# Where split weights lie in their buffers: byte offset 64 everywhere, or 88 and 76

## The chip, the core and the metric

The kernel runs on one core of one Trainium2 chip. Its time is the device time of one execution in microseconds (us); the time before is the median of three runs. A profiled execution gives the trace; its span goes from the first to the last instruction and is a little shorter than the execution's own time.

## The reference

One layer of a decoder trunk on x of 256 positions by 1024 channels, float32:

```python
proj = x @ w_in                      # 1024 x 10240: ten groups of 1024 columns
a_x, a_gate, s_u, s_v, q, k, v, g_a, g_s, g_m = split(proj)
y_a = rg_lru(causal_dwconv(a_x)) * gelu(a_gate)
y_s = gelu(s_u) * (tril(w_s) @ layer_norm(gelu(s_v)) + b)
y_m = moba_attention(q, k, v)        # 8 heads of 128; one block of 256, so causal
m = sigmoid(g_a)*y_a + sigmoid(g_s)*y_s + sigmoid(g_m)*y_m
x = layer_norm(alpha*x + m @ w_out)
h = x @ w_up                         # 1024 x 6144
x = layer_norm(alpha*x + (gelu(conv3(h_gate)) * h_up) @ w_down)
```

## The kernel before

All weights are streamed once from HBM, in chunks of 1 MiB (128 partitions x 2048 float32): 40 of w_in, 4 of w_out, 24 of w_up and 12 of w_down. A chunk of w_in or w_up holds 256 output columns for all eight blocks of 128 input channels, so a row of a partition is eight pieces of 256 floats, one after the other (index k).

To keep float32 accuracy with TensorE's float32r type, each operand is split in two: `split` (lines 68 to 70) lets ScalarE (ACT) write hi, the rounded copy, and VectorE (DVE) write lo, the rest. A product is then three matmuls, hi by hi, hi by lo and lo by hi (`passes`, line 125). A chunk thus costs 8 x 3 matmuls for each of two halves, 48 matmuls of 256 columns.

There are two ways to use a chunk. Feature-major (`fm_pe`, line 219): the weights are the stationary operand, 128 columns at a time, and the activations of all 256 positions (xh, xl, or x1Th, x1Tl for w_up) stream through; the result has channels on partitions. Token-major (`tm_mm`, line 240): 128 positions of the activations are stationary, and 256 weight columns stream. Token-major are the groups S_V and V of w_in and the first two gate chunks of w_up (`first_gates`, tile p_tg); the other 32 chunks of w_in (tiles p_ax, p_su, p_ag, p_gm, p_q, p_k, p_ga, p_gs) and 22 of w_up (p_g, p_u) are feature-major. Every one of these matmuls needs a weight load (LDWEIGHTS) of its own, a row PEld in the trace. w_out and w_down chunks stream 512 columns, or 256 in the last pieces p_woq and p_dq, against stationary activations (`row_mm`, line 631).

A step is a matmul function, the chunks it uses and a function that handles its results. The main loop (line 1015) loads up to LOOK = 3 chunks ahead on SP's DMA queue, prepares a chunk with `prep`, issues the matmuls and then the rest of the step. The order of TensorE's work is the order in the code; in three stretches that of the other engines is too. There are five raw buffers of half a chunk, four hi and four lo buffers.

A hi or lo buffer has 2048 + PAD elements, and `prep` (line 103) puts the chunk `shift_of` bytes into it, 4 bytes an element:

```python
at = shift_of.get(i, 0) // 4
hi = his.tile([P, 2048 + PAD], F32R, ...)[:, at : at + 2048]
lo = los.tile([P, 2048 + PAD], F32R, ...)[:, at : at + 2048]
```

`shifted(i)` (line 236) sets 64 bytes for each chunk of w_in and w_up; w_out and w_down are not in the table and lie at 0, and the activations are not shifted. So the shift sets the distance in a partition between what the weight load reads and what the matmul streams.

Of the kernel before, what the change touches and what calls it, by code (L numbers as in the profile page):

```python
# [31 lines left out]
A_X, A_G, S_U, S_V, Q_, K_, V_, G_A, G_S, G_M = range(10)  # L32
# [10 lines left out]
LOOK = 3  # L43


SHIFT = 64
PAD = 256


# [1 line left out]
def trunk_kernel(ctx: ExitStack, tc, xw, x, w_in, wrg, wsT, w_out, w_up, w_down, rows, packed, out):  # L51
# [23 lines left out]
    def chunk(src):  # L75
        chunks.append(src)
        return len(chunks) - 1

    shift_of = {}
# [153 lines left out]
        acts = cur["acts"]  # L233
        return pe

    def shifted(i):
        shift_of[i] = SHIFT
        return i

    def tm_mm(c, dst, tok, ks, acts, ms=(0, 1, 2)):  # L240
# [20 lines left out]
    def wi(group, c):  # L261
        return chunk(w_in[group * 4 + c])
# [3 lines left out]
    vst = small.tile([P, 2, 4, 6], F32, name="vst", tag="vst", bufs=1)  # L266

    def sv_step(c):
        i = shifted(wi(S_V, c))

        def pe():
            if c > 1:
                p = bank(f"p_sv{c}")
                cur["p"] = [p[:, 0, :], p[:, 1, :]]
                tm_pe(i, p)
                return
            cur["p"] = [bank(f"p_sv{c}{tok}")[:, 0, :] for tok in range(2)]
            for k in range(KT + 1):
                for ks, ms in (((k,), (0,)), ((k - 1,), (1, 2))):
                    for tok in range(2):  # L280
                        if 0 <= ks[0] < KT:
                            tm_mm(i, cur["p"][tok], tok, ks, (xh, xl), ms)

        def post():
            cols = slice(c * S, (c + 1) * S)
            for tok in range(2):
                nc.scalar.activation(va[:, tok, cols], cur["p"][tok], AF.Gelu_apprx_tanh)
                nc.vector.bn_stats(vst[:, tok, c, :], va[:, tok, cols])
            if c == 3:
                gb = U("gb", (P, 2, D))  # L290
                load_row(gb[:, 0, :], 0)
                load_row(gb[:, 1, :], 1)
                for tok in range(2):
                    mv, rs = aggregate(vst[:, tok], f"sv{tok}")
                    normalise(va[:, tok, :], va[:, tok, :], mv, rs, gb[:, 0, :], gb[:, 1, :])

        step(pe, [i], post)
# [34 lines left out]
    xc = {}  # L332

    def ax_step(c):
        i = shifted(wi(A_X, c))

        def pe():
            cur["p"] = p = bank(f"p_ax{c}")
            fm_pe(i, p)()

        def post():
            p = cur["p"]
            if c == 0:
                xc["f"] = U("xc")
                xc["h"] = U("xch", dt=F32R)
                xc["l"] = U("xcl", dt=F32R)
            for j in range(2):
                conv(xc["f"][:, 2 * c + j, :], p[:, j, :], "cw", "cb", 2 * c + j, 8, 4)
            s = slice(2 * c, 2 * c + 2)
            split(xc["f"][:, s, :], xc["h"][:, s, :], xc["l"][:, s, :])  # L350

        step(pe, [i], post)
# [1 line left out]
    gu = {}  # L354

    def su_step(c):
        i = shifted(wi(S_U, c))

        def pe():
            cur["p"] = p = bank(f"p_su{c}")  # L360
            fm_pe(i, p)()

        def post():
            if c == 0:
                gu["f"] = U("gu")
            nc.scalar.activation(gu["f"][:, 2 * c : 2 * c + 2, :], cur["p"], AF.Gelu_apprx_tanh)

        step(pe, [i], post)
# [23 lines left out]
    ga = {}  # L392

    def ag_step(c):
        i = shifted(wi(A_G, c))

        def pe():
            cur["p"] = p = bank(f"p_ag{c}")
            fm_pe(i, p)()

        def post():
            if c == 0:
                ga["f"] = U("ga")
            nc.scalar.activation(ga["f"][:, 2 * c : 2 * c + 2, :], cur["p"], AF.Gelu_apprx_tanh)

        step(pe, [i], post)
# [42 lines left out]
    sgm = {}  # L449

    def gm_step(c):
        i = shifted(wi(G_M, c))

        def pe():
            cur["p"] = p = bank(f"p_gm{c}")
            fm_pe(i, p)()

        def post():
            if c == 0:
                sgm["f"] = U("sgm")  # L460
            nc.scalar.activation(sgm["f"][:, 2 * c : 2 * c + 2, :], cur["p"], AF.Sigmoid)

        step(pe, [i], post)
# [1 line left out]
    av = {}  # L465

    def v_step(c):
        i = shifted(wi(V_, c))

        def pe():  # L470
            cur["p"] = p = bank(f"p_v{c}")
            tm_pe(i, p)

        def post():
            if c == 0:
                av["h"] = U("avh", (P, 2, D), F32R)
                av["l"] = U("avl", (P, 2, D), F32R)
                av["r"] = U("avr", (P, D))
            s = slice(c * S, (c + 1) * S)
            split(cur["p"], av["h"][:, :, s], av["l"][:, :, s])  # L480
            nc.scalar.copy(av["r"][:, s], cur["p"][:, 1, :])

        step(pe, [i], post)
# [1 line left out]
    qk = {}  # L485

    def qk_step(which, c):
        i = shifted(wi(Q_ if which == "q" else K_, c))

        def pe():  # L490
            cur["p"] = p = bank(f"p_{which}{c}")
            fm_pe(i, p)()

        def post():
            if which == "q":
                qk[c] = U(f"qk{c}", (P, 4, 2, S), F32R)
            o = 0 if which == "q" else 2
            hl = (qk[c][:, o], qk[c][:, o + 1])
            split(cur["p"], *hl)
            first = tmp.tile([P, 2, P], F32, name=f"{which}f{c}", tag=f"{which}f")  # L500
            nc.scalar.copy(first, cur["p"][:, :, :P])
            qk[which, c] = (*hl, first)

        step(pe, [i], post)
# [76 lines left out]
    mg = {}  # L581

    def ga_step(c):
        i = shifted(wi(G_A, c))

        def pe():
            cur["p"] = p = bank(f"p_ga{c}")
            fm_pe(i, p)()

        def post():  # L590
            s = slice(2 * c, 2 * c + 2)
            t = tmp.tile([P, 2, S], F32, name=f"sga{c}", tag="t0")
            nc.scalar.activation(t, cur["p"], AF.Sigmoid)
            nc.vector.tensor_mul(ga["f"][:, s, :], ga["f"][:, s, :], t)

        step(pe, [i], post)

    def gs_step(c):
        i = shifted(wi(G_S, c))

        def pe():
            cur["p"] = p = bank(f"p_gs{c}")
            fm_pe(i, p)()

        def post():
            if c == 0:
                mg["h"] = U("mgh", dt=F32R)
                mg["l"] = U("mgl", dt=F32R)
            s = slice(2 * c, 2 * c + 2)
            t = tmp.tile([P, 2, S], F32, name=f"sgs{c}", tag="t0")  # L610
            nc.scalar.activation(t, cur["p"], AF.Sigmoid)
            nc.vector.tensor_mul(t, t, gu["f"][:, s, :])
            nc.vector.tensor_add(t, t, ga["f"][:, s, :])
            nc.vector.tensor_add(t, t, sgm["f"][:, s, :])
            split(t, mg["h"][:, s, :], mg["l"][:, s, :])

        step(pe, [i], post)
# [129 lines left out]
    def up_chunk(which, c):  # L747
        return chunk(w_up[c if which == "g" else 12 + c])
# [6 lines left out]
        pf["t", c] = t  # L755

    def up_step(which, c):
        i = shifted(up_chunk(which, c))

        def pe():  # L760
            pf[which, c] = bank(f"p_{which}{c}")
            cur["acts"] = res["hl"]
            fm_pe(i, pf[which, c])()

        def post():
            if which == "g":
                gate_post(c)
                return
            t = pf["t", c]
            nc.vector.tensor_mul(t, t, pf["u", c])  # L770
            act = U(f"act{c}", (P, 2, 2, S), F32R)
            pf["a", c] = (act[:, 0], act[:, 1])
            split(t, *pf["a", c])

        step(pe, [i], post)

    def first_gates():


        ids = [shifted(up_chunk("g", c)) for c in range(2)]  # L780
        pairs = [(2 * q, 2 * q + 1) for q in range(4)]

        def mm(c, tok, ks):
            tm_mm(ids[c], pf["tm", c][:, tok, :], tok, ks, res["hl"])

        def open_pe():
            for c in range(2):
                pf["tm", c] = bank(f"p_tg{c}")
            mm(0, 0, range(KT))

        step(open_pe, ids)
        for q in range(4):
            def pe(q=q):
                mm(1, 0, pairs[q])
                x1t_pe(1, q, psb)

            step(pe, ids, lambda q=q: x1t_post(1, q))

        def evacuate(c):
            t = tmp.tile([P, 2, 384], F32, name=f"tg{c}", tag="prob")[:, :, :S]  # L800
            nc.scalar.copy(t, pf["tm", c])
            pf["tg", c] = t

        step(lambda: [mm(0, 1, ks) for ks in pairs], ids, lambda: evacuate(0))
        step(lambda: [mm(1, 1, ks) for ks in pairs], ids, lambda: evacuate(1))
# [114 lines left out]
    for c in range(4):  # L920
        sv_step(c)
# [172 lines left out]
```

## Time and profile before

| what | value |
|---|---|
| time, median of 3 runs | 485.58 us (485.13 to 487.52) |
| profiled execution, its own time | 485.5 us |
| its span | 483.8 us, granted TensorE clock 0.996 |
| busy: PE (matmul) / PEld (weight load) | 473.5 us / 458.1 us |
| busy: DVE / ACT / POOL | 337.3 / 271.4 / 21.9 us |
| read from HBM | 91.31 MB, 191 GB/s over the span with what is written |

Matmuls are pipelined: the duration of one in the trace is longer than the time to the start of the next. The pace is therefore read from starts: the time from the first start of a piece to the first start of the next piece, divided by the matmuls in the piece (their number is from the code, 48 per chunk; the counts of a window also hold those that only reach into it).

### The profile page before, as it was taken

What the parts mean: (1) busy time and instruction counts of PE and PEld (TensorE: products, weight loads), DVE (VectorE), ACT (ScalarE), POOL (GpSimd) and SP (SyncE); (2) the same over time, 40 slices, a digit from 0 to 9 for tenths busy, and PEclk for the clock granted to TensorE, in tenths of its full rate; (3) what the DMA queues carried; (4) which work ended last, traced back from release to release, by engine and by line L of the source; (5) the groups of instructions that cost most, each with busy time, mean ns of one, the idle gap of its engine ahead of it and who ended that gap; (6) DMA issues with size and microseconds to landing.
All of it is one profiled execution on the core that took longest, in us unless ns stands there. A gap on an engine that the chain in (4) does not pass through costs nothing.

```text
span 483.8 us, 9096 instructions
## 1 busy us (share of the span) xinstructions
PE 473.5 (98%) x3728; PEld 458.1 (95%) x3728; DVE 337.3 (70%) x527; ACT 271.4 (56%) x410; POOL 21.9 (5%) x24
## 2 busy tenths in 40 slices
PE   8999999999999999999999999999999999999993
PEld 7999999999999999999998899999999999999983
DVE  5889897464359979666685988766656566665635
ACT  6746764576489278666442378644444554444431
POOL 1021000000000000000001700000000000000003
PEclk9999999999999999999999999999999999999998
DMA  8997857474524496865452548875556555565002
GB/s 279 334 353 259 291 190 276 141 234 136 173 88 130 122 321 210 270 216 170 134 177 83 167 148 297 273 243 180 177 177 216 182 198 184 178 189 180 20 1 87
DMA packets 27385, 92.95 MB, mean 192 GB/s; under 512 B 3152, under 2 KB 3536, under 8 KB 27344
## 3 DMA queue, kind: packets, MB, share of 16 engines
q1 hardware_dynamic: 27344, 92.37, 57.8%
q8 instruction: 29, 0.48, 0.4%
q14 instruction: 12, 0.10, 0.1%
HBM read 91.31 MB, written 1.05 MB: 191 GB/s over the span
## 4 chain that ended last, share of the span: by engine, by line
issue 47%; PE 43%; DMA 3%; DVE 3%; ACT 1%; POOL 1%; SPq 1%; ACTq 0%; DVEq 0%; POOLq 0%
PE p_u L229 14%; PE p_d L638 13%; PE p_g L229 12%; DMA ws_raw<-in_wsT 2%; PE p_sv L247 2%; PE p_tg L247 2%; DMA xw<-in_xw 1%; DVE lo L70 1%; ACT hi L69 1%; PE p_dq L638 1%; SPq L93 0%; DVE st_m L193 0%; POOL rs_sv L201 0%; DVE x1Tl L70 0%; POOL rs_m L201 0%
## 5 line engine op out<-in xcount | busy, mean ns | idle before, releaser
L70 DVE TENSOR_TENSOR lo<-raw,hi 128x1024 fp32r<-128x1024 f32 (+1 forms) x162 | 189.1, 1191 | 74.7 <-ACT hi L69 73.8
L69 ACT CAST hi<-raw 128x1024 fp32r<-128x1024 f32 (+1 forms) x164 | 160.5, 1016 | 104.9 <-PE p_g L229 28.2
L638 PE MATMUL p_d<-hi,act 128*128 128x512 f32 x180 | 55.7, 391 | 0.0
L638 PEld LDWEIGHTS p_d<-hi,act 128*128 128x128 f32 x180 | 33.0, 188 | 6.3
L638 PE MATMUL p_d<-lo,act 128*128 128x512 f32 x90 | 35.0, 389 | 0.0
L329 DVE SCALAR_TENSOR_TENSOR cv<-p_g,par,cv 128x255 f32<-128x255 f32 (+1 forms) x48 | 23.0, 480 | 7.1 <-ACT cv L327 6.3
L229 PE MATMUL p_u<-x1Th,hi 128*128 128x256 f32 x192 | 26.6, 281 | 0.0
L229 PE MATMUL p_u<-x1Th,lo 128*128 128x256 f32 x192 | 26.4, 280 | 0.0
L229 PE MATMUL p_u<-x1Tl,hi 128*128 128x256 f32 x192 | 26.4, 280 | 0.0
L229 PEld LDWEIGHTS p_u<-x1Th,hi 128*128 128x128 f32 x192 | 25.0, 189 | 0.8
L327 ACT ACTIVATE cv<-p_g,par 128x256 f32<-128x256 f32 x24 | 13.5, 561 | 19.8 <-DVE cv L329 19.8
L229 PEld LDWEIGHTS p_u<-x1Th,lo 128*128 128x128 f32 x192 | 24.2, 189 | 0.0
L229 PEld LDWEIGHTS p_u<-x1Tl,hi 128*128 128x128 f32 x192 | 24.2, 189 | 0.0
L770 DVE TENSOR_TENSOR cv<-cv,p_u 128x512 f32<-128x512 f32 x12 | 8.2, 687 | 20.4 <-PE p_u L229 20.1
L229 PE MATMUL p_g<-x1Th,lo 128*128 128x256 f32 x160 | 22.0, 281 | 0.0
L229 PE MATMUL p_g<-x1Th,hi 128*128 128x256 f32 x160 | 22.0, 280 | 0.0
L229 PE MATMUL p_g<-x1Tl,hi 128*128 128x256 f32 x160 | 22.0, 280 | 0.0
L638 PEld LDWEIGHTS p_d<-lo,act 128*128 128x128 f32 x90 | 16.9, 188 | 3.6
L229 PEld LDWEIGHTS p_g<-x1Th,hi 128*128 128x128 f32 x160 | 20.2, 189 | 0.0
L229 PEld LDWEIGHTS p_g<-x1Th,lo 128*128 128x128 f32 x160 | 20.2, 189 | 0.0
L229 PEld LDWEIGHTS p_g<-x1Tl,hi 128*128 128x128 f32 x160 | 20.2, 189 | 0.0
L754 ACT ACTIVATE cv<-cv 128x512 f32<-128x512 f32 x12 | 7.6, 632 | 11.3 <-DVE cv L329 11.3
(241 smaller groups left out, 964.3 us busy)
## 6 DMA issues: line engine op xcount, KB each, us to landing
raw<-in_w_in SPq DMA_DIRECT2D x72, 512.0 KB, 5.2
raw<-in_w_up SPq DMA_DIRECT2D x48, 512.0 KB, 4.6
raw<-in_w_down SPq DMA_DIRECT2D x24, 512.0 KB, 4.7
raw<-in_w_out SPq DMA_DIRECT2D x8, 512.0 KB, 4.0
raw<-in_w_in SPq DMA_DIRECT2D x12, 256.0 KB, 5.8
xw<-in_xw SPq DMA_DIRECT2D x8, 256.0 KB, 5.1
gb<-in_rows SPq DMA_DIRECT2D x2, 512.0 KB, 8.3
rg_raw<-in_wrg SPq DMA_DIRECT2D x2, 512.0 KB, 7.0
```

Of the source, the lines that this page charges most:

```text
L69: nc.scalar.copy(hi, src)
L70: sub.tensor_sub(lo, src, hi.bitcast(F32))
L229: nc.tensor.matmul(dst[:, j, :], w[:, k, j * P : (j + 1) * P], a[:, k, :], start=(n == 0), stop=(n == 3 * KT - 1))
L247: nc.tensor.matmul(dst, a[:, k, tok * P : (tok + 1) * P], w[:, k, :], start=(m == 0 and k == 0), stop=(m == 2 and k == KT - 1))
L327: nc.scalar.activation(dst, src, AF.Identity, bias=pcol(bname, f), scale=w(taps - 1))
L329: nc.vector.scalar_tensor_tensor(dst[:, d:], src[:, : S - d], w(taps - 1 - d), dst[:, d:], op0=ALU.mult, op1=ALU.add)
L638: nc.tensor.matmul(dst, a[:, k0 + k, tok * P : (tok + 1) * P], w[:, k, s], start=(start and n == 0), stop=(stop and n == 6 * len(parts) - 1))
L754: nc.scalar.activation(t, t, AF.Gelu_apprx_tanh)
L770: nc.vector.tensor_mul(t, t, pf["u", c])
```

## The change

The single offset of 64 bytes becomes three, by the use of the chunk. `shifted` takes the offset as an argument:

```diff
-SHIFT = 64
+FM_IN, FM_UP, TM = 88, 76, 76
 PAD = 256
...
-    def shifted(i):
-        shift_of[i] = SHIFT
+    def shifted(i, by):
+        shift_of[i] = by
         return i
...
-        i = shifted(wi(S_V, c))              # sv_step; v_step alike
+        i = shifted(wi(S_V, c), TM)
...
-        i = shifted(wi(A_X, c))              # ax, su, ag, gm, q, k, ga, gs alike
+        i = shifted(wi(A_X, c), FM_IN)
...
-        i = shifted(up_chunk(which, c))      # up_step
+        i = shifted(up_chunk(which, c), FM_UP)
...
-        ids = [shifted(up_chunk("g", c)) for c in range(2)]      # first_gates
+        ids = [shifted(up_chunk("g", c), TM) for c in range(2)]
```

The 32 feature-major chunks of w_in then lie at 88 bytes, the 22 of w_up at 76, and the ten token-major chunks at 76. Nothing else differs.

## Rows read from the trace of the kernel before

**Rows 1.** The page: busy time (parts 1 and 2).

```profile
PE 473.5 (98%) x3728; PEld 458.1 (95%) x3728; DVE 337.3 (70%) x527; ACT 271.4 (56%) x410; POOL 21.9 (5%) x24
...
PE   8999999999999999999999999999999999999993
...
PEclk9999999999999999999999999999999999999998
```

**Rows 2.** The chain that ended last, 297 to 472 us: start, us, piece.

```profile
297.57 5.44 PE p_g L229 x48
...
308.48 5.65 PE p_u L229 x48
...
456.71 5.66 PE p_u L229 x48
462.37 9.55 PE p_d L638 x42
```

**Rows 3.** Stretches of w_in, PE alone: bounds, length, busy (instructions), clock, DMA share, GB/s.

```profile
29.44:51.21 21.77, 21.77 (x195) 1.00 0.85 306
...
105.23:110.89 5.66, 5.66 (x51) 1.00 0.74 237
...
126.51:149.13 22.62, 22.62 (x194) 1.00 0.29 95
...
184.87:196.25 11.38, 11.38 (x99) 1.00 0.71 226
199.16:210.55 11.39, 11.39 (x100) 1.00 0.90 325
...
226.58:232.32 5.74, 5.74 (x51) 1.00 0.54 171
233.41:249.83 16.42, 16.42 (x148) 1.00 0.49 160
```

**Rows 4.** Timeline of PE, p_sv: start, us, what, count.

```profile
18.13 1.10 PE L247 MATMUL p_sv<-hi,xh 128*128 128x256 f32 x8
...
28.50 1.10 PE L247 MATMUL p_sv<-lo,xh 128*128 128x256 f32 x8
```

**Rows 5.** Timeline of PE, p_dq on unshifted weights.

```profile
475.23 0.28 PE L638 MATMUL p_dq<-lo,act 128*128 128x256 f32 x1
...
475.59 0.28 PE L638 MATMUL p_dq<-lo,act 128*128 128x256 f32 x1
```

**Rows 6.** Timeline of PE, two entries into p_gs.

```profile
226.58 1.19 PE L229 MATMUL p_gs<-xh,hi 128*128 128x256 f32 x8
227.61 1.10 PE L229 MATMUL p_gs<-xl,hi 128*128 128x256 f32 x8
...
233.41 1.17 PE L229 MATMUL p_gs<-xh,hi 128*128 128x256 f32 x8
234.41 1.07 PE L229 MATMUL p_gs<-xl,hi 128*128 128x256 f32 x8
235.32 1.07 PE L229 MATMUL p_gs<-xh,lo 128*128 128x256 f32 x8
```

**Rows 7.** Groups of splits by form: busy us, mean ns, idle before and releasers.

```profile
L70 DVE TENSOR_TENSOR lo<-raw,hi 128x1024 fp32r<-128x1024 f32 x150 | 181.3, 1232 | 74.6 <-ACT hi L69 73.8 <-PE p_wo L638 0.3
...
L69 ACT CAST hi<-raw 128x1024 fp32r<-128x1024 f32 x152 | 153.7, 1047 | 104.3 <-PE p_g L229 28.2 <-PE p_u L229 21.2 <-DMA raw<-in_w_in 16.7
```

**Rows 8.** Stretches, all engines: PE, PEld, DVE, ACT, POOL, clock, DMA share, GB/s.

```profile
0.80:29.40 28.60, 27.37 (x226) 26.70 (x227) 21.42 (x40) 20.35 (x40) 1.53 (x7) 1.00 0.94 317
29.40:103.80 74.40, 74.40 (x659) 74.40 (x657) 60.73 (x97) 43.44 (x55) 4.15 (x3) 1.00 0.72 245
...
308.30:462.20 153.90, 153.90 (x1117) 145.73 (x1116) 92.72 (x111) 73.42 (x92) 0.00 (x0) 1.00 0.56 180
```

**Rows 9.** Timeline of PEld: p_t's weight loads, and the next.

```profile
225.90 0.69 PEld L552 LDWEIGHTS p_t<-ident,prob 128*128 128x128 f32 x6
226.56 0.30 PEld L229 LDWEIGHTS p_gs<-xh,hi 128*128 128x128 f32 x2
```

More of the change, by code (lines that the diff above doesn't have):

```diff
@@ L356, in su_step @@
     def su_step(c):
-        i = shifted(wi(S_U, c))
+        i = shifted(wi(S_U, c), FM_IN)
         def pe():
@@ L394, in ag_step @@
     def ag_step(c):
-        i = shifted(wi(A_G, c))
+        i = shifted(wi(A_G, c), FM_IN)
         def pe():
@@ L451, in gm_step @@
     def gm_step(c):
-        i = shifted(wi(G_M, c))
+        i = shifted(wi(G_M, c), FM_IN)
         def pe():
@@ L467, in v_step @@
     def v_step(c):
-        i = shifted(wi(V_, c))
+        i = shifted(wi(V_, c), TM)
         def pe():
@@ L487, in qk_step @@
     def qk_step(which, c):
-        i = shifted(wi(Q_ if which == "q" else K_, c))
+        i = shifted(wi(Q_ if which == "q" else K_, c), FM_IN)
         def pe():
@@ L583, in ga_step @@
     def ga_step(c):
-        i = shifted(wi(G_A, c))
+        i = shifted(wi(G_A, c), FM_IN)
         def pe():
@@ L598, in gs_step @@
     def gs_step(c):
-        i = shifted(wi(G_S, c))
+        i = shifted(wi(G_S, c), FM_IN)
         def pe():
```

## The prediction

> **What bounds the kernel now.** First the page: TensorE is busy 98% of the span and in nearly every slice, at full granted clock, and DVE and ACT are far below it [rows 1]. So I read next the chain that ended last: from 298 us to 472 us it is TensorE alone, piece after piece, and no DMA, DVE or ACT stands between the pieces [rows 2]. Nothing but TensorE's own pace, or the work it is given, can move this kernel by more than the few microseconds at its two ends. So I read the pace. One chunk of weights in feature-major or token-major form is 48 matmuls of 256 columns, each with a weight load of its own. The reader should see two things in the chain. The same 48 matmuls take 5.44 us in one place and 5.65 us in others, without any wait [rows 2]; that is 113.3 ns and 117.8 ns from start to start. And the piece of w_down, 42 matmuls of 512 columns on unshifted weights, takes 9.55 us, 227 ns each.
>
> The table by stage shows how this is spread over the first half [rows 3]. The stage of p_ax, 192 matmuls, takes 21.77 us, 113.4 ns each; p_gm after the first chunk takes 5.66 us per 48, 117.9; p_v takes 22.62 us for 192, 117.8; p_q and p_k of the last pair (96 matmuls in 11.38 us) and p_ga (two such stretches, 11.39 us the first) are at 118.5, a first slow matmul included; p_gs begins at the higher pace (226.58 to 232.32, 48 in 5.74 us) and ends at the lower one (144 in 16.42 us, 114.0 with one slow start). The token-major p_sv at the start goes from 18.13 to 28.50 us in 88 matmuls, 117.8 [rows 4]. Third, the unshifted reference of the same shape: p_dq starts three matmuls of 256 columns every 0.36 us, 120.0 ns each [rows 5]. Between 512 and 256 columns, both unshifted, lie 107 ns for 256 columns, so a matmul pays 13 ns over its columns without a shift, and 6.3 or 10.7 ns with the shift of 64 bytes. The place of the weights against the other operand thus has a price on this path, and one offset has two prices.
>
> Which of the two holds is settled on entry and then stays: p_gs starts after p_t with 8 matmuls in 1.03 us and goes on at the upper pace; its next chunk starts after p_o with 8 in 1.00 us and then does 8 in 0.91 us, the lower pace [rows 6]. By the chain and the table, 25 of the 64 shifted chunks run at the lower level (22 of w_in, 3 of w_up), 37 at the upper (10 of w_in's feature-major, 19 of w_up's, the 8 of p_sv and p_v), and the two p_tg chunks in between.
>
> **The change, part by part.** No instruction, DMA, wait or queue is added, removed or moved. All that differs is the byte at which ACT and DVE write hi and lo and at which TensorE reads them; 88 and 76 bytes are 22 and 19 elements, inside the 256 spare ones, so the edit does what it says. w_out and w_down keep offset 0: their matmuls stay at 227 and 120 ns.
>
> *Splits.* 64 chunks times four ACT and DVE instructions are written at another offset. The casts take 1047 ns and the subtractions 1232 ns on average [rows 7]. What they cost at an offset that is not a multiple of 64 bytes no row shows. From below: they could gain nothing that counts, as TensorE doesn't wait for them. From above: their cover is DVE's idle time. In the stretch 29.40 to 103.80 us DVE is busy 60.73 of 74.40 us, and in 308.30 to 462.20 us 92.72 of 153.90 [rows 8]. The first holds 28 subtractions, so each may grow by 13.67/28 = 0.49 us (40%) before DVE holds TensorE up; if it doubled, 28 x (1.23 - 0.49) = 21 us would be lost there. I take 0: the writes stay contiguous. What hides it is TensorE's 5.44 us per chunk against 2.5 us of subtraction.
>
> *Feature-major chunks of w_in at 88.* 32 chunks; 22 are at 5.44 us. The other ten stand 0.21 us higher each (5.65 - 5.44): 2.1 us if they come down.
>
> *w_up's chunks at 76.* 22 chunks in feature-major form, the three up to 303 us at the lower level (their pieces 5.44 to 5.48 us), the 19 from 308 us on at 5.65: 19 x 0.21 = 4.0 us.
>
> *Token-major chunks at 76.* Here the weights are the moving operand. p_v: 22.62 - 21.77 = 0.85 us. p_sv: its last two chunks 0.4 us; before 18 us DMA is 94% busy [rows 8] and I count nothing. p_tg: 0.1 us at most, counted in the range.
>
> So the sum with every shifted matmul at the lower level is 2.1 + 4.0 + 0.85 + 0.4 = 7.4 us. The pace that the new offsets really give is the unknown, and the trace bounds it on both sides. Lower end: six weight loads of p_t, whose matmuls are too short to hold them back, start 0.66 us before the load that follows them, 110 ns each [rows 9]; a pair of load and matmul can't go below that. Upper end: the unshifted 120.0 ns. Mean of the 3072 shifted matmuls now: 113.4 ns and the 7.4 us over it, 7400/3072 = 2.4, so 115.8 ns. At 110 everywhere, 3072 x 5.8 ns = 18 us are gained; at 120 everywhere, 3072 x 4.2 ns = 13 us are lost; at the upper level everywhere, 3072 x 2.0 = 6 us. I take the lower level, 113.4, since it is the nearest row: same shape, same operands, and it already holds in 25 chunks with an offset close by.
>
> What is late next: at 5.44 us per chunk nothing new. The stretch from 29.40 to 103.80 us already holds 13 chunks at that pace, with DVE at 82% and DMA at 72% [rows 8], and TensorE waits for neither; the later stretches have more room.
>
> The Trainium skill, TensorE: Matmul & The Clock Gate, in "Step-by-step: what each phase is for", says that the moving operand and the weight load have independent read ports, so that a load takes no bandwidth from the running matmul. By that rule the offset would be worth nothing, and the sum 0. This trace disagrees: 120.0 ns against 113.3 ns at the same shape [rows 2, 5].
>
> **Sum.** The profiled execution took 485.5 us (span 483.8), the median of the runs is 485.58, so the two agree. 485.5 - 7.4 = 478.1, rounded to 478.
>
> **Rivals.**
> *Below the lower level.* With offsets inside a 16-byte step (76) or off it (88) the two streams may meet less often than at 64. For it: one step, from 0 to 64, halved the 13 ns. Against: no row of a 256-column matmul is under 113. At 111.5, half-way to the load's 110: 3072 x 4.3 = 13.2 us, 472; at 110: 467.5. Chance 0.28.
> *No change.* The two levels follow from the entry, not from these bytes: the chunks keep their levels, 485.5, give or take 2. For it: one offset gives both levels. Against: 0 bytes gives neither. This is also where the rule of two ports would end. Chance 0.12.
> *Slower: the streams meet again.* One mechanism: at the new offsets the weight load's reads fall on the matmul's as they do at 0, and each matmul pays up to 13 ns. Its place is every shifted matmul; its price is 3072 times what the spacing exceeds 115.8 ns; it decides from there. At the upper level everywhere it gives 485.5 + 6 = 491.5; at 120, 498.5. For it: 37 of the 64 chunks already sit at the worse level of the present offset, and 25 at the better one have that to lose. Against: the offset stays away from 0, the one place where 120 is seen. Chance 0.20.
> The Trainium skill, SBUF — State Buffer, "Specifications", has 16-byte lines in SBUF with a penalty for each crossing to a new one. By it a row that starts 8 or 12 bytes into a line touches one line more, and the change would lose rather than gain; every offset in this trace is a multiple of 16, so no row here bears it out.
>
> **How the numbers follow.** Forecast 0.40, with its own range 474 to 482 (part of the chunks left above, or some a little below, the level). Below it 0.28, no change 0.12, slower 0.20. A measurement of this kernel tells about 0.5% from no change, 2.4 us. Faster: forecast and the first rival, 0.68. Same: 0.12. Slower: 0.20. The range reaches down to 466, just past the load's bound, and up to 488, past no change; the slower cases at 491.5 and 498.5 are the fifth left out.
>
> **What would show it.** In the chain after, the pieces of 48 from 308 us on at 5.44 us instead of 5.65, p_v at 21.8 us, p_gm and p_ga like p_ax, while w_down stays at 227 ns and p_dq at 120. Pieces of 5.3 us or less speak for the first rival, 5.76 us for the third; unchanged pieces of both lengths for the second. Casts or subtractions over 1.7 us with TensorE waiting for them would make my zero for the splits wrong.

## The result, and the profile after

480.59 us median of four runs (480.16 to 481.08) against 486.04 of the kernel before, run beside it (485.13 to 487.52): ratio 0.9885, 95% interval 0.9857 to 0.9913, about 1.1% faster. The profiled execution took 480.8 us, span 479.1, so 4.7 us less span than the profiled one before.

Busy times on the page, and DVE's and ACT's splits by form (busy us, mean ns, idle before and releasers), of the changed kernel. All its line numbers are one higher:

```profile
PE 468.3 (98%) x3728; PEld 453.0 (95%) x3728; DVE 337.0 (70%) x527; ACT 271.2 (57%) x410; POOL 21.8 (5%) x24
```

```profile
L71 DVE TENSOR_TENSOR lo<-raw,hi 128x1024 fp32r<-128x1024 f32 x150 | 181.2, 1233 | 69.9 <-ACT hi L70 69.5 <-PE p_wo L639 0.2
...
L70 ACT CAST hi<-raw 128x1024 fp32r<-128x1024 f32 x152 | 153.6, 1047 | 96.5 <-PE p_g L230 26.0 <-PE p_u L230 20.1 <-DMA raw<-in_w_in 15.6
```

Only TensorE lost busy time that counts: matmuls 5.2 us, weight loads 5.1. The splits cost what they did, 1233 and 1047 ns against 1232 and 1047 [rows 7], though they now start 8 or 12 bytes past a multiple of 16. The chain that ended last, from 297 us (start, us, piece):

```profile
296.79 5.44 PE p_g L230 x48
...
307.69 5.45 PE p_u L230 x48
313.14 5.44 PE p_g L230 x48
...
452.21 5.46 PE p_u L230 x48
457.67 9.54 PE p_d L639 x42
467.21 4.32 PE p_dq L639 x36
```

All 19 pieces of w_up from 308 us on went from 5.65 us to between 5.44 and 5.46 [rows 2]; w_down's piece of 42 stayed (9.54 against 9.55). By their starts the 19 take 3.9 us less in all, of the 4.7. The first half by stretches, PE alone (length, busy, clock, DMA share, GB/s), with the answers to [rows 3] in order; q1 and k1 (the second chunks of p_q and p_k, fourth and fifth row) and p_tg's last piece are added:

```profile
29.46:51.24 21.78, 21.78 (x195) 1.00 0.80 292
...
105.37:110.97 5.60, 5.60 (x51) 1.00 0.68 237
126.49:149.06 22.57, 22.57 (x194) 1.00 0.29 95
159.96:165.67 5.71, 5.71 (x50) 1.00 0.34 103
165.67:171.27 5.60, 5.60 (x50) 1.00 0.85 263
185.07:196.08 11.01, 11.01 (x100) 1.00 0.71 230
198.98:209.98 11.00, 11.00 (x99) 1.00 0.91 329
225.63:231.31 5.68, 5.68 (x51) 1.00 0.57 169
232.40:248.85 16.45, 16.45 (x148) 1.00 0.51 162
279.10:284.79 5.69, 5.69 (x51) 1.00 0.29 78
```

The same three added stretches in the kernel before:

```profile
160.02:165.64 5.62, 5.62 (x50) 1.00 0.36 110
165.64:171.09 5.45, 5.45 (x51) 1.00 0.89 248
280.05:285.58 5.53, 5.53 (x51) 1.00 0.25 73
```

The four p_ga chunks (11.39 to 11.00 us for each two) and q3, k3 (11.38 to 11.01) came down. The three p_gm chunks after p_ri hardly did: 5.60 us, 116.7 ns, a level that the kernel before did not show. p_v went from 117.8 to 117.6 ns. Two parts became slower. In q1 TensorE is held up for some 0.2 us, as it was before; behind that, q1's second half and k1 run at 116.7 ns, where they ran at 113.3. The last p_tg piece takes 5.69 us instead of 5.53: 116.7 ns instead of 113.3.

Neither TensorE's clock nor DMA orders these paces. The granted clock is 1.00 in every row; before, 113.4 ns stood beside a DMA share of 0.85 (p_ax) and 117.8 beside 0.29 (p_v) [rows 3].

### The profile page after: what moved, and what is told of

It is laid out like the page before. It is cut to its first block, busy times and chain, and to the rows that moved or that the text cites. A ratio compares the mean times of both kernels' runs of the same rounds, so it can differ in the third digit from the quotient of the medians.

```text
span 479.1 us, 9096 instructions
## 1 busy us (share of the span) xinstructions
PE 468.3 (98%) x3728; PEld 453.0 (95%) x3728; DVE 337.0 (70%) x527; ACT 271.2 (57%) x410; POOL 21.8 (5%) x24
## 4 chain that ended last, share of the span: by engine, by line
issue 47%; PE 41%; DVE 3%; POOL 1%; ACT 1%; ACTq 0%; DVEq 0%; POOLq 0%
PE p_u L230 14%; PE p_d L639 13%; PE p_g L230 11%; PE p_tg L248 2%; PE p_dq L639 1%; POOL rs_sv L202 1%; ACT hi L70 1%; DVE lo L71 0%; DVE va L207 0%; DVE st_m L194 0%; DVE x1Tl L71 0%; POOL rs_m L202 0%; DVE x L687 0%; PE p_x1t L679 0%; PE p_g L813 0%
```

## The experiments

A pace is the time from one matmul's start to the next; an entry is the work that a stretch of such matmuls follows (w_down's p_d, the recurrence gates' p_ri, the attention's transposes p_t, p_mix, or p_sv). Three theories were to be told apart. Theory A: the distance in bytes between what the weight load reads and what the matmul streams sets which paces are stable; where there are two, the stream keeps the one it entered. Theory B: the pace is drawn at each entry, and the bytes only redraw it. Theory C, for the scans: what counts is where the weights start, inside a step of 16 bytes or in memory, not the distance. The runs e4, e6 to e8, e10 and e12 were each executed once, with the profiler: they are read for paces, not for times.

**One class at a time.**

```diff
+FM_IN, FM_UP, TM = 64, 76, 64   # e1
+FM_IN, FM_UP, TM = 88, 64, 64   # e2
+FM_IN, FM_UP, TM = 64, 64, 76   # e3
```

> Only w_up's feature-major chunks move, to 76; all others stay at 64. Theory A (the offset sets the pace, chunk by chunk): the pieces of 48 from 308 us on take 5.45 us instead of 5.65, everything before 285 us is as in the kernel before; 4.0 us faster, about 481.7 (ratio 0.992). Theory B (the pace is drawn anew at each entry and the bytes only redraw it): pieces at 5.44 and 5.65 mixed after 308 us, gain between 0 and 4 us.

> Only w_in's 32 feature-major chunks move, to 88; all others stay at 64. Theory A: q3, k3 and the four p_ga at 113.3 ns, p_gm after its first chunk at 116.7, half of q1 and k1 at 116.7 as in the changed kernel, p_up as before: 1.3 us faster, about 484.6 (ratio 0.997). Theory B: the stages that change level are other ones than in the changed kernel, 2 us faster to 1 us slower.

> Only the ten token-major chunks move, to 76. Theory A: p_v 117.6 ns instead of 117.8, the last part of p_tg 5.69 us instead of 5.53: no gain or 0.1 us loss, about 486 (ratio 1.000). Theory B: w_up's or w_in's stages change level without an edit of theirs, up to 4 us either way.

e1: ratio 0.9929 (0.9904 to 0.9954); e2: 0.997 (0.9947 to 0.9992); e3: 0.9973 (0.9954 to 0.9991). A pair of w_up's pieces in the chain of e1, then of e2:

```profile
311.16 5.46 PE p_u L230 x48
316.62 5.44 PE p_g L230 x48
```

```profile
309.32 5.66 PE p_u L230 x48
314.97 5.65 PE p_g L230 x48
```

In e1's chain the 19 pieces of w_up alternate so, and in e2's and e3's they are all at 5.65 or 5.66. So w_up's own offset sets w_up's pace, as theory A has it. But in e1 a stage without an edit changed. The stretch of p_ax in e1, then in e2, PE alone:

```profile
29.42:52.03 22.61, 22.61 (x194) 1.00 0.82 299
```

```profile
29.37:51.77 22.40, 22.40 (x195) 1.00 0.80 292
```

In e1 the same bytes, 64, run p_ax at 117.8 ns, where the profile before has 21.77 us and 113.4 [rows 3]. e1's nine runs fall apart in two lots, 481.2 to 481.4 (near the 481.7 expected) and 483.4 to 484.9. The 13 chunks from 29 to 104 us are 624 matmuls; at 4.4 ns that is 2.8 us, about the gap between the lots. So at 64 bytes that stretch has two paces, and I read the lots as the two, from one execution to the next. At 88 it has two as well: 113.4 ns in the changed kernel and 116.7 in e2. This is what theory B said, for these offsets. It also makes e2's ratio no proof of theory A: the 0.997 is as expected, but not the trace behind it, where q3, k3 and p_ga gain and the stretch of 13 chunks takes 2.0 us more than in the profile before.

e3's ratio is below 1, though 1.000 was expected and it saves nothing in the trace; its runs reach only 486.3, the ones beside it 490.35. I read that as p_sv at 76, which comes just ahead, leading p_ax into the lower pace. The profiles bear it out: with p_sv at 76 and p_ax at 64 or 88, p_ax is at 113.4 or 113.5 ns in all eight (the changed kernel, e3, e4, e6, e7, e8, e10, e12); with p_sv at 64 it is in one of three (before, but not e1 and e2).

**A scan inside one kernel.** Each pair of w_up chunks (u_c, then g_c+1 without a break) is entered after the same 24 matmuls of w_down, so one run times ten offsets. The runs also give p_gm, p_v and p_ga offsets of their own.

```diff
-        i = shifted(up_chunk(which, c), FM_UP)
+        i = shifted(up_chunk(which, c), UP_AT.get(c if which == "u" else c - 1, FM_UP))
```

> Changed kernel with one offset per pair of w_up chunks (u_c, g_c+1), c = 2 to 11, each entered after the same 24 matmuls of w_down: 0, 16, 32, 48, 64, 80, 96, 112, 128, 192. Also p_gm 1 to 3 at 0, 32, 76; p_v 0 to 3 at 0, 32, 52, 116; p_ga first pair at 0, second at 64. Theory A: the pace is a function of the offset that repeats: 120.0 ns at 0 and at 128 or before, 117.8 at 64 and 192, the others each at a fixed level between 110 and 120. Theory B: all offsets but 0 give 113.3 or 117.8 without an order in the bytes. Theory C (the start inside a 16-byte line matters, not the line): all of these, multiples of 16, at the same 117.8 or 120.

> As the scan in steps of 16, with w_up's pairs at 4, 8, 12, 20, 24, 28, 36, 40, 44, 52; p_gm 1 to 3 at 24, 40, 104; p_v at 4, 12, 24, 40; p_ga at 24, then 76. Theory C (the start inside a 16-byte line decides): 12, 28, 44 at 113.3 like 76, which is 12 bytes into its line; 8, 24, 40 at 116.7 like 88. Theory A (a function of the whole distance, with a period of 64 or 128): 12 at 113.3 if the period is 64, and 24 like 88; 28 and 44 at values of their own.

> The same with w_up's pairs at 56, 60, 68, 72, 76, 84, 88, 92, 100, 104; p_gm at 64, 72, 80; p_v at 64, 88, 100, 112; p_ga at 40, then 104. Theory C: 60, 76, 92 at 113.3; 56, 72, 88, 104 at 116.7. Theory A: 76 at 113.3 and 64 (p_gm) at 117.8 as before, a smooth change between neighbours, 72 and 84 near 76's value.

Some rows of their chains, e4 at 0 and 64, then e6 at 8 and 24, then e7 at 72, 76, 84, 88 (the u chunk of each; their g chunks agree):

```profile
309.61 5.75 PE p_u L234 x48
...
377.12 5.66 PE p_u L234 x48
```

```profile
326.20 5.55 PE p_u L234 x48
...
376.43 5.84 PE p_u L234 x48
```

```profile
359.80 5.68 PE p_u L234 x48
...
376.62 5.45 PE p_u L234 x48
...
392.99 5.76 PE p_u L234 x48
...
409.99 5.46 PE p_u L234 x48
```

From the starts, the pace over the last 32 matmuls of the g chunks (of u11 at 52, 104 and 192), in ns:

| offset | pace | offset | pace | offset | pace |
|---|---|---|---|---|---|
| 0 | 120.0 | 36 | 119.9 | 76 | **113.3** |
| 4 | 118.2 | 40 | 119.1 | 80 | 118.6 |
| 8 | 115.5 | 44 | 117.9 | 84 | 119.9 |
| 12 | 116.5 | 48 | 118.3 | 88 | **113.3** |
| 16 | 118.3 | 52 | 120.1 | 92 | 118.3 |
| 20 | 120.1 | 56 | 118.0 | 96 | 117.3 |
| 24 | 121.3 | 60 | 119.7 | 100 | 120.0 |
| 28 | 116.7 | 64 | 117.8 | 104 | 117.7 |
| 32 | 118.3 | 68 | 118.4 | 112, 128 | 120.1, 120.2 |
|  |  | 72 | 118.2 | 192 | 117.7 |

Of 30 offsets, 76 and 88 alone reach 113.3 after w_down, and none goes below. Theory C falls: 12, 28, 44, 60 and 92 are all 12 bytes past a multiple of 16 like 76, and run at 116.5 to 119.7. A period of 64 falls too (12 is not 76, 24 is not 88); the two pairs 128 bytes apart, 0 and 128, 64 and 192, agree within 0.2 ns. The smooth change between neighbours that theory A was given for e7 is not there either: 72 and 84 run at 118.2 and 119.9, beside 113.3 at 76.

With another entry most offsets keep their pace. p_gm, entered after p_ri, gave 120.0 at 0, 118.2 at 32, 118.7 at 80 and 113.5 at 76. Two do not: 104 ran at 120.0 in p_gm of e6 (117.7 in the table), and 24 at 118.7 in its p_ga, entered after p_t (121.3 in the table). So these have two paces, like 64 and 88. The stretch of that p_ga, two chunks, PE alone:

```profile
200.23:211.70 11.47, 11.47 (x99) 1.00 0.94 323
```

In token-major form p_v ran its four chunks of e7 at 117.8 ns (at 64 bytes), 120.0 (88), 120.8 (100) and 113.3 (112); the last two of them (windows of PE alone, each with a few matmuls of its neighbours):

```profile
138.47:144.28 5.81, 5.81 (x51) 1.00 0.05 21
144.28:149.75 5.47, 5.47 (x51) 1.00 0.03 8
```

Of the 18 offsets that p_v had in all runs, 112 alone reached 113.3.

**The distance or the place.** The streamed activations x1T are moved as well. PAD is 128 in these two runs, so the buffers' sizes differ too.

```diff
-            res["hl"] = [U(f"x1T{x}", dt=F32R) for x in "hl"]
+            res["hl"] = [up.tile([P, KT * S + 64], F32R, name=f"x1T{x}", tag="U")[
+                :, X1_AT // 4 : X1_AT // 4 + KT * S].rearrange("p (k m) -> p k m", m=S) for x in "hl"]
```

> The activations x1T, which stream in w_up's feature-major matmuls, lie at 76 bytes too, and w_up's pairs at 76, 152, 140, 128, 92, 64, 88, 100, 116, 172, so their distances are 0, 76, 64, 52, 16, -12, 12, 24, 40, 96. (Also p_gm at 60, 68, 92; p_v at 20, 56, 72, 84; p_ga at 12, then 60.) Theory A (distance alone): 120.0 ns at distance 0, 113.3 at 76, 117.8 at 64, 118.3 at 16, 117.3 at 96. Theory C (the weights' own place in a line): 113.3 at the weights' places 76, 140, 92 and 172, 117.8 or more at 128 and 64.

> As the run with shifted activations, but x1T at 64 bytes, a multiple of 16, and w_up's pairs at 140, 152, 128, 64, 76, 88, 144, 80, 72, 124: distances 76, 88, 64, 0, 12, 24, 80, 16, 8, 60. Theory A (distance, for a stream that starts on a 16-byte line): the paces of the scan at the same distances, 113.3 at 76 and 88, 117.8 at 64, 120.0 at 0, 116.7 at 12, 121.5 at 24, 118.6 at 80, 118.3 at 16, 115.5 at 8, 119.4 at 60. Theory C (the places of both in memory, not their distance): the weights' places 76 and 88 at 113.3 again, or another order altogether.

With x1T at 64 (e12), chains at distances 76, 88, 64, 0, 12 (weights at 140, 152, 128, 64, 76):

```profile
313.62 5.44 PE p_g L235 x48
...
330.00 5.44 PE p_g L235 x48
...
346.58 5.66 PE p_g L235 x48
...
363.43 5.76 PE p_g L235 x48
...
380.28 5.60 PE p_g L235 x48
```

Weights at 140 and 152 run at 113.3 ns, and weights at 76, at distance 12, at 116.7. The other distances of e12 gave 118.6 (24), 118.9 (80), 118.3 (16), 115.6 (8) and 119.2 (60); but for 24 each is within 0.5 ns of the table, and 118.6 is the other pace of 24, the one of p_ga in e6. So with the stream unshifted or shifted by 64 bytes the distance decides, not the weights' place. With x1T at 76 (e8) the distance alone does not: of the nine distances that the table has too, three agree within 0.3 ns (120.0 at 0, 118.3 at 16, 117.5 at 64) and six do not, among them 118.0 at 76 and 120.0 at 96. A stream that starts at 76 bytes has another map. What makes the difference, no run here tells.

**Whether a pace is kept.** Two offsets in one pair.

```diff
+UP_AT = {"u": {2: 76, 3: 64, 4: 76, 5: 76, 6: 88, 7: 0, 8: 8, 9: 76, 10: 76, 11: 88},
+         "g": {2: 64, 3: 76, 4: 0, 5: 88, 6: 64, 7: 76, 8: 76, 9: 80, 10: 72}}
```

> Two offsets in each pair of w_up chunks, u then g without a break: 76 then 64; 64 then 76; 76 then 0; 76 then 88; 88 then 64; 0 then 76; 8 then 76; 76 then 80; 76 then 72; and u11 at 88. Also p_gm 1 to 3 at 8, 76, 64, p_v at 112, 64, 48, 112, p_ga at 8, then 12. Theory A (a stable pace is a state that the stream holds, and 64 has two): 64 after 76 or after 88 stays at 113.3, where 64 after w_down ran at 117.8; 76 falls to 113.3 from 64, 0 and 8; 0, 80 and 72 go to 120.0, 118.6 and 118.3 also from the lower pace. Theory B (the byte alone): 64 at 117.8 also after 76.

The chain of e10, pairs 76 then 64, 64 then 76, 76 then 0, 88 then 64, 0 then 76:

```profile
307.53 5.46 PE p_u L234 x48
312.98 5.44 PE p_g L234 x48
318.42 5.46 PE p_d L643 x24
323.89 5.66 PE p_u L234 x48
329.54 5.44 PE p_g L234 x48
...
340.45 5.46 PE p_u L234 x48
345.90 5.76 PE p_g L234 x48
...
373.49 5.46 PE p_u L234 x48
378.95 5.44 PE p_g L234 x48
...
389.86 5.75 PE p_u L234 x48
395.61 5.45 PE p_g L234 x48
```

At 64 bytes a chunk takes 5.66 us after w_down and 5.44 us after a chunk at 76 or 88, in one and the same execution. 76 takes 5.44 or 5.45 us after 64, 0 and 8 alike; 0, 80 and 72 go up at once even from the lower pace. This is what theory A said, for feature-major chunks. In token-major form the same run has p_v at 64 bytes behind a chunk of it at 112: it went from 113.3 up to 117.8 ns, so there 64 did not keep the lower pace.

**One chunk to lead the others.**

```diff
+FM_IN, FM_UP, TM = 64, 64, 64
...
-        i = shifted(wi(A_X, c), FM_IN)
+        i = shifted(wi(A_X, c), 76 if c == 0 else FM_IN)
```

> The kernel before with one edit: the first A_X chunk lies at 76, all other shifted ones at 64. Theory A: the stretch of 13 chunks from 29 to 104 us is led into the lower pace in every execution and stays there at 64; its runs lie within 1 us at about 485.5, where those of the kernel before reach 2.8 us (624 matmuls by 4.4 ns) and more above that; ratio 0.997. Theory B: some runs still 2.8 us longer, ratio 1.000.

Ratio 0.9968 (0.995 to 0.9985), twelve runs from 484.56 to 486.21, 1.65 us where 1 was expected; the seventeen beside them go from 485.36 to 489.31. Its profile has p_ax at 113.4 ns. One chunk of 80 at another offset is worth 0.3%; that it does so by holding the stretch of 13 chunks at the lower pace fits the narrower times and rests on this one profile.

**Two versions beyond the change.**

```diff
+FM_IN, FM_UP, TM = 76, 76, 76    # e5
+FM_IN, FM_UP, TM = 76, 76, 112   # e9
```

> Changed kernel with w_in's feature-major chunks at 76 too. p_gm 3 ran at 113.5 ns with 76 after p_ri, where 88 gives 116.7 and 64 gives 117.8. Theory A (76 has no upper level that is stable after these entries): p_gm, q1, k1 and gs0 all at 113.3, and the stretch 29 to 104 us at 113.4 in every execution; 0.9 us faster than the changed kernel where that had the lower level there, about 479.7, and the runs within 1 us of each other. Theory B (drawn anew at each entry): some stage at another level, 480 to 483.

> All feature-major chunks at 76, the token-major ones at 112, where the last chunk of p_v ran at 113.3 ns in the scan. Theory A (112 pulls p_v and p_sv down from any entry): p_v 0.8 us shorter than with 76, p_sv up to 0.7 us, p_tg 0.2 us; about 478.5, ratio to the kernel before 0.981. Theory B (112 held 113.3 only because of the chunk ahead of it): p_v at another level, 479.5 to 481.

e5: 479.88 us, ratio to the kernel before 0.9836 (0.9809 to 0.9862); p_gm 1 to 3 are at 113.5 ns, k1 at 113.4, gs0 (the first chunk of p_gs) at 5.53 us, as theory A said, and p_tg's last piece is still at 5.69. e9: 478.89 us, ratio 0.9848 (0.9819 to 0.9877), where 0.981 was expected. The two intervals overlap, so the runs don't part e5 from e9; the trace does. Stretches, PE alone: p_gm 1 of e5, then p_v and q1 of e9:

```profile
104.73:110.18 5.45, 5.45 (x50) 1.00 0.66 223
```

```profile
125.15:146.97 21.82, 21.82 (x194) 1.00 0.29 98
157.90:164.16 6.26, 5.71 (x51) 1.00 0.29 96
```

and the weight load that waited in q1 (us in total, times, longest):

```profile
PEld p_q L230 <- DVE lo L71: 0.7, 1, 0.7
```

p_v came down to 113.6 ns, 0.75 us less than in the changed kernel, and q1 gave 0.55 of it back: its weight load now waits for a subtraction, which DVE does only after the recurrence (line 446). That is the next limit in this stage.

## Why the prediction was right, point by point

The mechanism of the forecast is the one found: nothing changed but the time from one matmul to the next, and no chunk went below the lower level. w_up's term held: 4.0 us forecast, 3.9 measured, and e1 shows that its edit alone gives it. The splits at nothing held. Of the signs that it listed, w_up's 5.44 us, p_ga at the lower level and w_down and p_dq as before all came; p_v at 21.8 us and p_gm like p_ax did not.

Two terms were too large. For w_in 2.1 us stood in the sum; p_ga, q3 and k3 gave 1.1 us and p_gm with gs0 0.2, while q1 and k1 lost 0.3 after a short wait: 1.0 net. The token-major term of 1.25 us came to nothing: p_v gave 0.05 us, p_sv's last chunks under 0.05, and p_tg lost 0.16. The step that failed is to take one level, 113.4 ns, for all three classes. For the chunks of w_in, 88 has an upper pace of its own, 116.7. In token-major form 76 is not a good offset: it ran at 117.5 ns in p_v and the later half of p_sv, at 116.7 in p_tg's last piece, and nowhere at 113.3, while 112 does (e9). There the weights are the moving operand and the distance has the other sign; that the sign is the reason, no run shows. With these terms 7.4 us becomes 4.8, and the span shows 4.7.

That w_up's term came out was in part luck. The level was taken as the nearest row, "with an offset close by", and closeness is no guide: 72, 80 and 84 are nearer to 76 than 64 is, and run at 118.2 to 119.9.

The rival of no change was part true: at 64 and 88 entry does decide. It was wrong for 76 in feature-major form, which reached 113.3 from every entry that it had here. The slower rival was nearer than its 0.20 looks: 27 of 30 offsets, all but 8, 76 and 88, run at 116.5 ns or more after w_down, over the 115.8 from which the change would have lost. The rival below the lower level has no run for it. The Trainium skill, SBUF — State Buffer, "Specifications", has lines of 16 bytes and a penalty for each crossing to a new one. That rule does not order these paces: 76 and 88 start inside a line and are the best, 64 and 80 start on one and run at 117.8 and 118.6 ns.

The median before was itself not one number: 29 to 104 us at 64 bytes has two paces, 2.8 us apart. The profile before happened to hold the lower one; the forecast counted it as sure. So the token-major edit, worth nothing in its own matmuls, has a use that the forecast did not see: behind p_sv at 76 that stretch was at the lower pace in every profile, and e3's 0.3% has no other source in its trace. The 26 runs beside e1 to e3 spread over 5.3 us, more than 2.8; what makes the rest is not shown.

## What to carry to other kernels

Where weight loads and matmuls follow each other closely, read the pace from the starts, piece by piece: one shape at two paces without a wait is a state of the stream, and an offset of the weights can choose it. Scan offsets inside one kernel, each entered in the same way, and take one that reaches the lower pace from every entry that the kernel has (76 here, feature-major) rather than one that only keeps it (64). Do it per use, since weights that move and weights that stand want different offsets (112 and 76 here), and again when the other operand moves.

## What was unexpected

Between 113.3 and 121.3 ns per matmul of 256 columns, 7%, is set by where the weights lie against the stream, and of 30 distances two are good after w_down. At 64 bytes either pace lasts through 13 chunks and 75 us, p_mix's eight matmuls between them notwithstanding: the upper in e1, the lower in the profile before; after p_ri both are at the upper. Why these distances, the runs don't show.
